# Gate and up products of two feed-forward halves by seven block products instead of eight, with blocks of 256 tokens

## The chip, the cores and the metric

The kernel runs on one core of a Trainium2 chip. The metric is the device time of one execution in microseconds (us), the median over several runs. TensorE (PE) does the matrix products into PSUM; VectorE (DVE), ScalarE (ACT) and GpSimd (POOL) do the element-wise work; SyncE (SP) issues the transfers.

## The reference

Two layers over 1024 tokens with 1024 features: a recurrent block (Hawk) in layer 0, an RWKV-7 time mixing in layer 1, and after each a dense feed-forward and a gated per-layer embedding ("ple"). The change touches the feed-forward:

```python
def swiglu(x, w_in, w_out):
    gu = x @ w_in
    gate, up = jnp.split(gu, 2, axis=-1)
    return (jax.nn.silu(gate) * up) @ w_out
...
    h = h + swiglu(rms_norm(h, norm_ffn[i]), ffn_w_in[i], ffn_w_out[i])
    ple = (p[i] @ ple_w_proj[i]) * jax.nn.sigmoid(rms_norm(h, norm_ple[i]) @ ple_w_gate[i])
    h = h + ple
```

The inner width of the feed-forward is 2816, which is 22 tiles of 128.

## The kernel before

Features lie on the 128 partitions and tokens along the free dimension. The 1024 tokens are two halves of 512 (index t), so each layer has two feed-forward halves, four in all. The features of one half are eight tiles (index k).

Every product is made exact enough by splitting both operands into a high part (rounded to the matmul's type) and a low part (the remainder): `mm3` issues three matmuls for each k, high by high, high by low and low by high, each with a 128x128 weight and 512 columns. A weight tile arrives in `raw` (SP's queue), ScalarE casts its high part into `whl` and GpSimd subtracts to get the low part (`load_w`, L238 and L239). In the two regions where a second half of the hidden state fits beside the first (`extra`), `raw` has 2+2 buffers and `whl` 4+4.

A feed-forward half (`ffn`) goes over the 22 tiles f in groups of 2, 4, 4, 4, 4, 4. For each f it makes the gate product `pg` and the up product `pu` (24 matmuls each), then `silu(pg) * pu`, split into the tile `hid`. After each group the output products `ops` (`out_proj`, eight columns n, three matmuls for each f of the group) are added into the hidden state h (L390). In the last group the squares of h are summed as well (L301), and the norm for the next stage starts (`nxt`).

A norm for the whole half (`norm_xn`) needs one matmul `nps` that sums over the partitions, two activations that give `rstd`, and then for each k one multiply on VectorE (L317) and one split (cast on ScalarE, subtraction on VectorE, L290). Where `raw` is given (`raw_x`), the unnormed h is split instead, and `rstd` is applied behind the product.

The scheduler of the framework fixes each engine's order when the program is built, by priorities in program order and by its own idea of what is ready; on the chip each engine takes its instructions strictly in that order. Two of the four feed-forward halves concern us: the first half of layer 0, behind Hawk, and the second half of layer 1, near the end.

## Time and profile before

| | |
|---|---|
| median of 3 runs | 3099.32 us |
| lowest and highest | 3097.59 and 3109.37 us |
| the profiled execution, its own time | 3106.82 us |
| its span | 3105.0 us |
| matmuls in it | 16904 |
| PE busy in the span | 2958.3 us |

The span runs from the first to the last instruction; the profiled execution's own time is 1.8 us above it. A matmul's busy time is modelled, since matmuls overlap; what one costs in a row of them is read from the distance of starts.

### The profile page before, as it was taken

Reading aid. Unit: us, or ns where it says so; the run is one execution under the profiler, and the core shown is the slowest. Engines: PE = TensorE matmul, PEld = TensorE weight load, DVE = VectorE, ACT = ScalarE, POOL = GpSimd, SP = SyncE. Lnnn points to the kernel's source line nnn. Section 1 sums busy time; section 2 is a strip of 40 time slices with the busy share of each in tenths; the row PEclk is TensorE's granted clock in tenths of the full one; section 3 lists DMA queues with packets and bytes.
Section 4 is the critical chain, followed back from the end, with each engine's and each line's share of the span. In section 5 each row is a group of like instructions: output and inputs, shape, how many; then the busy total and the mean of one; then the engine's idle time right before and its main releaser. Section 6 shows DMA issues by size and latency. Waiting matters only on the chain. (4 is left out here: it accounts for less than half of the span.)

```text
span 3105.0 us, 45886 instructions
## 1 busy us (share of the span) xinstructions
PE 2958.3 (95%) x16904; PEld 2292.7 (74%) x16904; DVE 1677.9 (54%) x2950; ACT 1438.3 (46%) x2565; POOL 1282.7 (41%) x1080
## 2 busy tenths in 40 slices
PE   5999999999999999999998999999999999999998
PEld 3777778888776777777776667776767777888886
DVE  8756771111563266576678565777866456222145
ACT  5564752222555443444465774454344445322244
POOL 5111134444445444343434344434333355544445
PEclk9999999999998999999999999999999999999999
DMA  3211123333335464333323366423323252333323
GB/s 126 60 36 53 50 79 105 94 94 95 98 126 179 158 190 128 89 111 98 114 91 98 119 204 198 125 85 111 100 88 100 70 185 91 103 95 95 95 81 109
DMA packets 223968, 336.04 MB, mean 108 GB/s; under 512 B 56960, under 2 KB 75136, under 8 KB 223744
## 3 DMA queue, kind: packets, MB, share of 16 engines
q1 hardware_dynamic: 223456, 332.75, 34.9%
q8 instruction: 133, 2.18, 0.3%
q14 instruction: 91, 0.75, 0.1%
q10 hardware_dynamic: 288, 0.37, 0.0%
HBM read 278.24 MB, written 54.79 MB: 107 GB/s over the span
## 5 line engine op out<-in xcount | busy, mean ns | idle before, releaser
L239 POOL TENSOR_TENSOR whl<-raw,whl 128x512 fp32r<-128x512 f32 (+2 forms) x818 | 1061.8, 1303 | 1410.4 <-ACT whl L238 1319.8
L238 ACT CAST whl<-raw 128x512 fp32r<-128x512 f32 (+2 forms) x818 | 482.2, 593 | 851.5 <-PE ops L115 226.2
L115 PE MATMUL ops<-hid,whl 128*128 128x512 f32 x2112 | 523.8, 401 | 13.8 <-DVE hid L290 6.4
L115 PE MATMUL pg<-xn,whl 128*128 128x512 f32 (+1 forms) x2184 | 522.9, 392 | 4.4 <-ACT whl L238 1.9
L115 PEld LDWEIGHTS pg<-xn,whl 128*128 128x128 f32 x2184 | 405.2, 188 | 98.9 <-issue 4.3
L115 PEld LDWEIGHTS ops<-hid,whl 128*128 128x128 f32 x2112 | 392.6, 189 | 113.8 <-DVE hid L290 12.5
L115 PE MATMUL pu<-xn,whl 128*128 128x512 f32 x1584 | 385.9, 396 | 3.1 <-ACT xn L289 1.4
L115 PEld LDWEIGHTS pu<-xn,whl 128*128 128x128 f32 x1584 | 296.0, 189 | 72.0 <-DVE xn L290 2.1
L115 PE MATMUL pps<-mix,whl 128*128 128x512 f32 x1152 | 301.3, 412 | 11.9 <-ACT mix L289 5.1
L390 DVE TENSOR_TENSOR h<-h,ops 128x512 f32<-128x512 f32 x256 | 173.9, 685 | 210.6 <-PE ops L115 208.7
L555 DVE TENSOR_TENSOR sg<-sg,pu 128x512 f32<-128x512 f32 x88 | 60.4, 686 | 396.0 <-PE pu L115 395.4
L115 PEld LDWEIGHTS pps<-mix,whl 128*128 128x128 f32 x1152 | 217.7, 193 | 75.1 <-issue 7.7
L115 PE MATMUL pg<-raw,whl 128*128 128x512 f32 x720 | 198.0, 415 | 0.0
L115 PEld LDWEIGHTS pg<-raw,whl 128*128 128x128 f32 x720 | 134.4, 193 | 34.4 <-issue 3.8
L241 POOL TENSOR_SCALAR whl<-raw 128x512 fp32r<-128x512 f32 (+2 forms) x84 | 58.7, 704 | 217.6 <-PE rps L115 69.7
L115 PE MATMUL pu<-raw,whl 128*128 128x512 f32 x528 | 141.4, 406 | 0.0
L115 PE MATMUL rps<-xn,whl 128*128 128x512 f32 x480 | 123.4, 405 | 16.3 <-ACT xn L289 10.5
L115 PEld LDWEIGHTS rps<-xn,whl 128*128 128x128 f32 x480 | 91.9, 193 | 42.8 <-issue 12.0
L115 PE MATMUL gps<-xn,whl 128*128 128x512 f32 x480 | 117.9, 400 | 0.0
L115 PE MATMUL ops<-m,whl 128*128 128x512 f32 x480 | 114.4, 396 | 0.8 <-ACT m L289 0.8
L115 PEld LDWEIGHTS pu<-raw,whl 128*128 128x128 f32 x528 | 96.1, 188 | 23.8 <-issue 2.6
L115 PEld LDWEIGHTS gps<-xn,whl 128*128 128x128 f32 x480 | 92.3, 192 | 21.4 <-issue 0.5
(277 smaller groups left out, 4027.2 us busy)
## 6 DMA issues: line engine op xcount, KB each, us to landing
raw<-in_ffn_in SPq DMA_DIRECT2D x352, 256.0 KB, 2.6
raw<-in_ffn_out SPq DMA_DIRECT2D x152, 256.0 KB, 2.6
raw<-in_rkv SPq DMA_DIRECT2D x96, 256.0 KB, 3.0
raw<-in_ple_gate SPq DMA_DIRECT2D x64, 256.0 KB, 2.6
raw<-in_w_in SPq DMA_DIRECT2D x48, 256.0 KB, 2.8
h<-h SPq DMA_DIRECT2D x32, 256.0 KB, 3.5
raw<-in_ffn_out SPq DMA_DIRECT2D x48, 128.0 KB, 2.1
raw<-in_w_o SPq DMA_DIRECT2D x24, 256.0 KB, 2.7
```

The lines of the kernel that those rows point to most:

```text
L115: self.nc.tensor.matmul(out, lhsT=lhsT, rhs=rhs, start=start, stop=stop)
L238: nc.scalar.copy(hl[:rows, 0, :w], raw[:rows, :w])
L239: nc.gpsimd.tensor_sub(hl[:rows, 1, :w], raw[:rows, :w], hl[:rows, 0, :w].bitcast(F32))
L241: nc.gpsimd.tensor_scalar(hl[:rows, 0, :w], raw[:rows, :w], 1.0, 0.0, ALU.mult, ALU.add)
L390: nc.vector.tensor_add(hs, hs, ps)
L555: nc.vector.tensor_mul(sg, sg, pu)
```

## The change

The gate and up products of one f are seen as a 2x2 block product: rows gate and up, inner blocks k = 0..3 and k = 4..7, columns the first and the last 256 tokens. `ffn_s` makes it with seven block products (`prod`, each 4 k x 3 matmuls of 256 columns), with Winograd's order of sums. The sums of weight blocks (S1 to S4) are made by VectorE for every f in `strassen_w`, and seven weight blocks are split instead of four tiles. The sums of activation blocks (T1 to T4) are made once for each half in `norm_s`. The products share three PSUM tiles `sA`, `sB` and `sC`, whose intermediate values are copied or added out in 256-column pieces; the last two products of an f are done between those of the next f. The output products of a group are issued behind the first f of the next group.

Around it: Hawk's end no longer norms the second half, which `norm_later` does during the last output products of the first half. In layer 1 the ple columns of half 0 are no longer split around the feed-forward of half 1, and the norm ahead of the last ple is applied behind the product (`raw`), for which `ple_last` multiplies by `rn`. `raw` and `whl` get 2+4 and 4+7 buffers, and one more activation tile is there in the second region. 

```diff
-            raw = self.ring("raw", [128, 512], F32, 2, 2)
+            raw = self.ring("raw", [128, 512], F32, 2, 4)
...
-            hl = self.ring("whl", [128, 2, 512], F32R, 4, 4)
+            hl = self.ring("whl", [128, 2, 512], F32R, 4, 7)
...
+    def norm_later(self, t, gname, gi, keep=False):
+        r = self.rstd(t)
+        self.rn[t] = None
+        xn = [self.xq("xn", "xb") for _ in range(4)]
+        self.xn[t] = xn
+        def some(k0):
+            for k in (k0, k0 + 1):
...
+    def norm_s(self, t, gname, gi):
+        nc = self.nc
+        r = self.rstd(t)
+        self.rn[t] = None
+        b11 = self.xq("xs", "xb")
+        t12 = [self.xq("xs", "xb") for _ in range(2)]
+        b2 = [self.xq("xs", "xb"), self.xq("xs")]
+        t34 = [self.xq("xs", "xb"), self.xq("xs", "hid")] if self.nxb > 4 else [self.xq("xs") for _ in range(2)]
+        def two(x):
+            return x.rearrange("p (b s) -> p b s", s=TH // 2)
+        def put(dst, src, lo):
+            nc.scalar.copy(dst[0], src)
+            lo.tensor_sub(dst[1], src, dst[0].bitcast(F32))
+        a, b = slice(0, TH // 2), slice(TH // 2, TH)
+        for k in range(4):
+            x, y, u, v = (self.t2("xn") for _ in range(4))
+            self.scaled(x, k, t, gname, gi, r)
+            self.scaled(y, k + 4, t, gname, gi, r)
+            q = b11.rearrange("p i a (b s) -> p i (a b) s", s=TH // 2)
+            put([q[:, i, k, :] for i in range(2)], x[:, a], nc.vector)
+            nc.vector.tensor_sub(u[:, a], x[:, b], x[:, a])
+            nc.vector.tensor_sub(u[:, b], y[:, b], u[:, a])
+            nc.gpsimd.tensor_sub(v[:, a], y[:, b], x[:, b])
+            nc.vector.tensor_sub(v[:, b], y[:, a], u[:, b])
+            for q, src, lo in ((t12, u, nc.vector), (b2, y, nc.vector), (t34, v, nc.gpsimd)):
+                q = q[k // 2].rearrange("p i a (b s) -> p i a b s", s=TH // 2)
+                put([q[:, i, :, k % 2, :] for i in range(2)], two(src), lo)
...
+    def strassen_w(self, g, u):
+        nc = self.nc
+        g0, u0, u1, g1 = raw = [self.ring("raw", [128, 512], F32, 2, 4) for _ in range(4)]
+        for x, src in zip(raw, (g[:, 0:512], u[:, 0:512], u[:, 512:1024], g[:, 512:1024])):
+            nc.sync.dma_start(x, src)
+        s1, s2, s3, s4 = (self.te("ws") for _ in range(4))
+        def split(x, lo):
+            hl = self.ring("whl", [128, 2, 512], F32R, 4, 7)
+            nc.scalar.copy(hl[:, 0, :], x)
+            lo.tensor_sub(hl[:, 1, :], x, hl[:, 0, :].bitcast(F32))
+            return lambda k, i: hl[:, i, k * 128 : k * 128 + 128]
+        w = {"A11": split(g0, nc.gpsimd)}
+        nc.vector.tensor_add(s1, u0, u1)
+        w["S1"] = split(s1, nc.gpsimd)
+        nc.vector.tensor_sub(s2, s1, g0)
+        w["S2"] = split(s2, nc.vector)
+        nc.vector.tensor_sub(s4, g1, s2)
+        w["A12"] = split(g1, nc.gpsimd)
+        w["S4"] = split(s4, nc.vector)
+        nc.vector.tensor_sub(s3, g0, u0)
+        w["S3"] = split(s3, nc.gpsimd)
+        w["A22"] = split(u1, nc.gpsimd)
+        return w
+    def ffn_s(self, l, t, nxt, groups, mid=None, raw=None):
+        nc, A = self.nc, self.A
+        a, b = slice(0, TH // 2), slice(TH // 2, TH)
+        def prod(ps, w, x, start, stop):
+            for k in range(4):
+                wh, wl, xh, xl = w(k, 0), w(k, 1), x(k, 0), x(k, 1)
+                for i, (p, q) in enumerate(((wh, xh), (wh, xl), (wl, xh))):
+                    nc.tensor.matmul(ps[:, a], lhsT=p, rhs=q, start=start and k + i == 0, stop=stop and k == 3 and i == 2,
+                                     skip_group_check=True)
...
+        def finish(last):
+            w, pa, s4, sg, fq, fj = last
+            def seven():
+                prod(pa, w["S3"], X["T3"], False, False)
+                nc.vector.tensor_add(s4[:, a], pa[:, a], s4[:, a])
+            def four():
+                prod(pa, w["A22"], X["T4"], False, True)
+                nc.vector.tensor_mul(sg[:, b], sg[:, b], s4[:, a])
+                nc.vector.tensor_mul(sg[:, a], sg[:, a], pa[:, a])
+                self.split(fq[:, 0, fj, :], fq[:, 1, fj, :], sg)
+            return seven, four
...
+        for g in groups:
+            for i in range(g):
+                if i % 2 == 0:
+                    q = self.xq("hid", "hid" if nq % 2 and self.nxb == 4 else None)
+                    nq += 1
+                hd[f + i] = q, i % 2
+                w = self.strassen_w(A["ffn_in"][l, f + i], A["ffn_in"][l, NF + f + i])
+                pa, pb, pc = self.ps("sA"), self.ps("sB"), self.ps("sC")
+                st, s4, sg = (self.t2(x) for x in ("st", "s4", "sg"))
+                seven, four = finish(hold) if hold else (lambda: None,) * 2
+                prod(pa, w["A11"], X["B11"], True, False)
+                nc.scalar.copy(st[:, a], pa[:, a])
+                seven()
+                prod(pb, w["S1"], X["T1"], True, False)
+                nc.scalar.copy(s4[:, a], pb[:, a])
+                prod(pa, w["S2"], X["T2"], False, False)
+                nc.scalar.copy(st[:, b], pa[:, a])
+                four()
+                prod(pc, w["A12"], X["B21"], True, True)
+                nc.vector.tensor_add(sg[:, a], pc[:, a], st[:, a])
+                prod(pb, w["S4"], X["B22"], False, True)
+                nc.vector.tensor_add(sg[:, b], pb[:, a], st[:, b])
+                nc.scalar.activation(sg, sg, AF.Silu)
+                hold = w, pa, s4, sg, q, i % 2
+                if todo is not None:
+                    out(*todo)
+                    todo = None
+            todo = f, g, f + g == NF
+            f += g
+        seven, four = finish(hold)
+        seven()
+        four()
+        if mid is not None:
+            mid()
+        out(*todo)
...
-            nc.scalar.activation(sg, pg, AF.Exp, scale=-1.0)
+            nc.vector.tensor_mul(sg, pg, self.rn[t][:, s])
+            nc.scalar.activation(sg, sg, AF.Exp, scale=-1.0)
...
-        K.hawk(lambda t: K.norm_xn(t, "norm_ffn", 0, t == 1))
+        K.hawk(lambda t: K.norm_s(t, "norm_ffn", 0) if t == 0 else None)
...
-        K.ffn(0, (0,), norm_ple)
+        K.ffn_s(0, 0, norm_ple, (2, 4, 4, 4, 4, 4), lambda: K.norm_later(1, "norm_ffn", 0, True))
...
-    extra(ctx)
+    extra(ctx, 5)
...
-    K.rwkv_out(1, 0, KD, True, lambda t: K.norm_xn(t, "norm_ffn", 8))
-    K.ple(1, (0,), K.final, ph, 0, 4)
-    K.ffn(1, (1,), lambda t: K.norm_xn(t, "norm_ple", 8))
-    K.ple(1, (0,), K.final, ph, 4, KD)
+    K.rwkv_out(1, 0, KD, True, lambda t: K.norm_s(t, "norm_ffn", 8))
+    K.ple(1, (0,), K.final, ph)
+    K.ffn_s(1, 1, lambda t: K.raw_norm(t, False), (2, 4, 4, 4, 4, 4), raw=("norm_ple", 8))
```

The order shows what moves on PE. In the middle of a feed-forward half of before, PE has two products of 24 matmuls for each f, and `ops` behind four f:

```order
L115 MATMUL pg<-xn,whl 128x512 x24
L115 MATMUL pu<-xn,whl 128x512 x24
L115 MATMUL pg<-xn,whl 128x512 x24
L115 MATMUL pu<-xn,whl 128x512 x24
L115 MATMUL ops<-hid,whl 128x512 x96
```

In the change the output products of a group stand behind the first f of the next; then comes one f: 24 matmuls into `sA` (the first product of this f and the sixth of the one before), 12 into `sB`, 24 into `sA` (the third of this, the last of the one before), and 12 each into `sC` and `sB`:

```order
L115 MATMUL ops<-hid,whl 128x512 x96
L660 MATMUL sA<-xs,whl 128x256 x24
L660 MATMUL sB<-xs,whl 128x256 x12
L660 MATMUL sA<-xs,whl 128x256 x24
L660 MATMUL sC<-xs,whl 128x256 x12
L660 MATMUL sB<-xs,whl 128x256 x12
```

So an f has 84 matmuls of 256 columns where it had 48 of 512.

At the end of Hawk's output products (`ops<-m`, the last four columns of the second half), where the first feed-forward half begins, PE has before:

```order
L115 MATMUL ops<-m,whl 128x512 x38
L115 MATMUL pu<-xn,whl 128x512 x36
L115 MATMUL nps<-acc,ones 128x512
L115 MATMUL pg<-xn,whl 128x512 x48
L115 MATMUL pu<-xn,whl 128x512 x12
L115 MATMUL ops<-hid,whl 128x512 x48
```

and in the change, where `xs` are the activation blocks from `norm_s`:

```order
L115 MATMUL ops<-m,whl 128x512 x38
L660 MATMUL sA<-xs,whl 128x256 x6
L660 MATMUL sB<-xs,whl 128x256 x3
L660 MATMUL sC<-xs,whl 128x256 x3
L660 MATMUL sB<-xs,whl 128x256
L660 MATMUL sC<-xs,whl 128x256 x3
L660 MATMUL sA<-xs,whl 128x256 x4
L660 MATMUL sB<-xs,whl 128x256 x2
L660 MATMUL sA<-xs,whl 128x256 x2
L660 MATMUL sB<-xs,whl 128x256 x5
L660 MATMUL sA<-xs,whl 128x256 x2
L660 MATMUL sB<-xs,whl 128x256
```

The products of the first two f are interleaved there, and the `nps` of the second half has gone from this place; it stands behind the last f of the half.

On VectorE the same place (h_93 is the second half's hidden state, h_86 the first's) reads before:

```order
L390 TENSOR_TENSOR h_93<-h_93,ops 128x512
L317 SCALAR_TENSOR_TENSOR xn<-h_86,vec,rstd 128x512 x3
L290 TENSOR_TENSOR xn<-xn 128x512 x3
L317 SCALAR_TENSOR_TENSOR xn<-h_86,vec,rstd 128x512 x3
L290 TENSOR_TENSOR xn<-xn 128x512 x3
L317 SCALAR_TENSOR_TENSOR xn<-h_86,vec,rstd 128x512 x2
L301 TENSOR_TENSOR acc<-acc,sq 128x512
L290 TENSOR_TENSOR xn<-xn 128x512 x2
```

and in the change the same norm is mixed with the block sums (L608 to L611) and the low parts of seven blocks (L599); of its four rounds this is the first and the start of the second:

```order
L407 TENSOR_TENSOR h_93<-h_93,ops 128x512
L317 SCALAR_TENSOR_TENSOR xn<-h_86,vec,rstd 128x512 x2
L599 TENSOR_TENSOR xs<-xn,xs 128x256
L608 TENSOR_TENSOR xn<-xn 128x256
L407 TENSOR_TENSOR h_93<-h_93,ops 128x512
L609 TENSOR_TENSOR xn<-xn 128x256
L317 SCALAR_TENSOR_TENSOR xn<-h_86,vec,rstd 128x512
L611 TENSOR_TENSOR xn<-xn 128x256
L599 TENSOR_TENSOR xs<-xn,xs 128x2x256 x2
L317 SCALAR_TENSOR_TENSOR xn<-h_86,vec,rstd 128x512
L599 TENSOR_TENSOR xs<-xn,xs 128x256
L608 TENSOR_TENSOR xn<-xn 128x256
```

What was 16 instructions of 512 columns for the eight k is now 16 of 512 and 16 of 256 columns, with three of the four `h_93` additions between them.

## Rows read from the trace of the kernel before

**Rows 1.** The page: busy us (share of the span) and instructions of each engine.

```profile
PE 2958.3 (95%) x16904; PEld 2292.7 (74%) x16904; DVE 1677.9 (54%) x2950; ACT 1438.3 (46%) x2565; POOL 1282.7 (41%) x1080
```

**Rows 2.** Windows: busy us (instructions) in two stretches, granted clock, DMA share, GB/s.

```profile
400.00:500.00 100.00, 97.66 (x408) 77.12 (x407) 54.27 (x72) 44.77 (x76) 42.21 (x33) 0.98 0.32 100
...
2700.00:2800.00 100.00, 99.21 (x435) 81.16 (x434) 19.96 (x25) 29.02 (x48) 47.05 (x37) 1.00 0.31 95
```

**Rows 3.** Timeline of PE, one group of four f: start, us, xcount [idle before].

```profile
2739.97 5.66 PE L115 MATMUL pg<-xn,whl 128*128 128x512 f32 x24
2745.46 5.60 PE L115 MATMUL pu<-xn,whl 128*128 128x512 f32 x24
...
2783.70 2.46 PE L115 MATMUL ops<-hid,whl 128*128 128x512 f32 x10
2786.55 19.88 PE L115 MATMUL ops<-hid,whl 128*128 128x512 f32 x86 [0.39 <-DVE hid L290]
2806.27 5.66 PE L115 MATMUL pg<-xn,whl 128*128 128x512 f32 x24
```

**Rows 4.** Timeline of the last us, where matmuls have 256 columns.

```profile
3084.25 3.01 PE L115 MATMUL pg<-xn,whl 128*128 128x256 f32 x24
...
3087.09 0.86 PE L115 MATMUL pq<-ph,whl 128*128 128x256 f32 x6
3087.79 0.59 PE L115 MATMUL nps<-acc,ones 128*128 128x256 f32 x2
...
3089.32 0.42 DVE L635 TENSOR_TENSOR sg<-sg,pq 128x256 f32<-128x256 f32 x1 [2.00 <-ACT sg L634]
```

**Rows 5.** Groups by line and shape, PE: busy us, mean ns.

```profile
L115 PE MATMUL pg<-xn,whl 128*128 128x256 f32 x48 | 6.5, 288 | 0.0
```

**Rows 6.** The same view of POOL, ACT and DVE: busy us, mean ns | idle before.

```profile
L239 POOL TENSOR_TENSOR whl<-raw,whl 128x512 fp32r<-128x512 f32 x718 | 976.2, 1364 | 1257.0 <-ACT whl L238 1183.2 <-issue 28.8 <-DVE h L390 13.8
```
```profile
L238 ACT CAST whl<-raw 128x512 fp32r<-128x512 f32 x718 | 442.0, 618 | 777.4 <-PE ops L115 208.9 <-PE pu L115 123.1 <-PE pg L115 108.7
...
L238 ACT CAST whl<-raw 128x256 fp32r<-128x256 f32 x96 | 38.1, 402 | 73.1 <-PE ops L115 17.3 <-PE pg L115 16.8 <-DMA raw<-in_w_o 14.7
```
```profile
L390 DVE TENSOR_TENSOR h<-h,ops 128x512 f32<-128x512 f32 x256 | 173.9, 685 | 210.6 <-PE ops L115 208.7
```

**Rows 7.** Timeline of POOL and DVE inside a feed-forward half, layer 0.

```profile
745.87 1.30 POOL L239 TENSOR_TENSOR whl<-raw,whl 128x512 fp32r<-128x512 f32 x1 [1.46 <-ACT whl L238]
...
746.57 1.14 DVE L290 TENSOR_TENSOR hid<-sg,hid 128x512 fp32r<-128x512 f32 x1 [0.69 <-ACT hid L289]
```

**Rows 8.** Timeline of PE, then DVE, then POOL: Hawk's end, first feed-forward half.

```profile
417.68 9.38 PE L115 MATMUL ops<-m,whl 128*128 128x512 f32 x38
426.89 4.56 PE L115 MATMUL pu<-xn,whl 128*128 128x512 f32 x18
432.90 0.50 PE L115 MATMUL pu<-xn,whl 128*128 128x512 f32 x1 [1.44 <-ACT xn L289]
434.12 0.96 PE L115 MATMUL pu<-xn,whl 128*128 128x512 f32 x3 [0.71 <-DVE xn L290]
```
```profile
404.71 0.68 DVE L390 TENSOR_TENSOR h<-h,ops 128x512 f32<-128x512 f32 x1
...
420.10 2.68 DVE L317 SCALAR_TENSOR_TENSOR xn<-h,vec,rstd 128x512 f32<-128x512 f32 x3 [0.66 <-ACT rstd L313]
422.70 1.89 DVE L290 TENSOR_TENSOR xn<-xn 128x512 fp32r<-128x512 f32 x3
424.50 4.19 DVE L317 SCALAR_TENSOR_TENSOR xn<-h,vec,rstd 128x512 f32<-128x512 f32 x3
...
433.38 1.82 DVE L290 TENSOR_TENSOR xn<-xn 128x512 fp32r<-128x512 f32 x2
```
```profile
404.65 1.30 POOL L239 TENSOR_TENSOR whl<-raw,whl 128x512 fp32r<-128x512 f32 x1 [2.46 <-ACT whl L238]
...
423.36 4.11 POOL L239 TENSOR_TENSOR whl<-raw,whl 128x512 fp32r<-128x512 f32 x2 [2.46 <-ACT whl L238]
```

More of the change, by code (lines that the diff above doesn't have):

```diff
@@ L204, in xq @@
             return self.xp.tile([128, 2, 2, TH], F32R, tag="xq", name=nm, bufs=6)
-        return self.ep.tile([128, 2, 2, TH], F32R, tag=ext, name=nm, bufs={"xb": 4, "hid": 2}[ext])
+        return self.ep.tile([128, 2, 2, TH], F32R, tag=ext, name=nm, bufs={"xb": self.nxb, "hid": 2}[ext])
     def ring(self, tag, shape, dt, bufs, more):
@@ L330, in norm_xn @@
         self.pause(4500)
+    def norm_later(self, t, gname, gi, keep=False):
[5 more added lines that the diff above has]
+            for k in (k0, k0 + 1):
+                x = self.t2("xn")
+                self.scaled(x, k, t, gname, gi, r)
+                if keep:
+                    self.nc.sync.dma_start(self.xn_d[k], x)
+                self.split(*self.xs(k, t), x)
+        self.items = [lambda k0=k0: some(k0) for k0 in range(0, KD, 2)]
     def raw_x(self, k, t, gname, gi):
@@ L562, in ffn, with pair @@
             f0 += g
+    def norm_s(self, t, gname, gi):
[14 more added lines that the diff above has]
+            x, y, u, v = (self.t2("xn") for _ in range(4))
+            self.scaled(x, k, t, gname, gi, r)
+            self.scaled(y, k + 4, t, gname, gi, r)
[8 more added lines that the diff above has]
+                put([q[:, i, :, k % 2, :] for i in range(2)], two(src), lo)
+        def pair(q, j):
+            return lambda k, i: q[k // 2].rearrange("p i a (b s) -> p i a b s", s=TH // 2)[:, i, j, k % 2, :]
+        self.xsb = {
+            "B11": lambda k, i: b11.rearrange("p i a (b s) -> p i (a b) s", s=TH // 2)[:, i, k, :],
+            "T1": pair(t12, 0), "T2": pair(t12, 1), "B21": pair(b2, 0), "B22": pair(b2, 1),
+            "T3": pair(t34, 0), "T4": pair(t34, 1),
+        }
@@ new lines, in ffn_s, with out @@
+    def ffn_s(self, l, t, nxt, groups, mid=None, raw=None):
[7 more added lines that the diff above has]
+                                     skip_group_check=True)
+        X = self.xsb
+        f, hd, hold, todo = 0, {}, None, None
+        def finish(last):
[9 more added lines that the diff above has]
+            return seven, four
+        def out(f0, g, last):
+            self.out_proj(
+                lambda n: self.load_w(A["ffn_out"][l, n, :, f0 * 128 : (f0 + g) * 128], g * 128),
+                g, lambda k, t: (hd[f0 + k][0][:, 0, hd[f0 + k][1], :], hd[f0 + k][0][:, 1, hd[f0 + k][1], :]),
+                (t,), last=last, nxt=nxt, raw=raw if last else None)
+        nq = 0
+        for g in groups:
[33 more added lines that the diff above has]
+        out(*todo)
@@ L569, in ple_in @@
             s = slice(t * TH, (t + 1) * TH)
-            q = self.xq("ph", "hid" if len(ts) == 2 and t == 1 else None)
+            q = self.xq("ph", "hid" if self.ep is not None and t == 1 else None)
             for k in range(2):
@@ L1298, in tile_trunk, with extra @@
     nc = tc.nc
-    def extra(c):
+    def extra(c, nxb=4):
+        K.nxb = nxb
         K.ep = c.enter_context(tc.tile_pool(name="ep", bufs=1))
@@ L1442 @@
     arrays = layout({k: np.asarray(v) for k, v in inputs.items()})
-    nc = bacc.Bacc("TRN2", target_bir_lowering=False, num_devices=1)
+    nc = bacc.Bacc("TRN2", target_bir_lowering=False, num_devices=1, dynamic_dma_scratch_size=1024)
     A = {n: nc.dram_tensor("in_" + n, a.shape, mybir.dt.from_np(a.dtype), kind="ExternalInput").ap()
```

## The prediction

> **What bounds the kernel now.** I read the page's busy shares first: PE is busy for 95% of the span, every other engine for 54% or less [rows 1]. Then the windows: in the middle of a feed-forward half PE is at 99% and at the full clock, while DVE has 20%, ACT 29%, POOL 47% and the transfers 31% of their time [rows 2]. So in the two halves that change PE alone sets the pace, and what a matmul costs there is read from the distance of starts, since busy times overlap. Two products of 24 matmuls start 5.49 us apart; four f take 2783.70 - 2739.97 = 43.73 us, so one f 10.93 us; the group with its 96 output matmuls takes 66.30 us [rows 3]. That is 228 ns for 512 columns. PE waits only 0.39 us in the group, for the low part of the last `hid`.
>
> **The gain on PE.** The order shows 84 matmuls of 256 columns for each f in place of 48 of 512, and 22 f in each of two halves, 44 in all. Half as many columns pay only if such a matmul costs about half. The trace has some at its very end: 24 take 3087.09 - 3084.25 = 2.84 us, 118.3 ns each, and the next six 0.70 us, 117 ns each [rows 4]. With 118.3 ns an f costs 9.94 us, 0.99 less, and 44 of them give **-43.7 us**. The bounds: exactly half of the 512-column distance, 113.9 ns, gives 9.57 us and -60 us. The busy time of the group of 48 divided by its count, 135 ns [rows 5], which counts edges and gaps twice, gives 11.34 us and +18 us. I take the distance of starts of the 24, because they are the same kind of stream and long enough. A rule of the Trainium skill speaks against the change: the page TensorE: Matmul & The Clock Gate, section "Why this matters for your kernels", wants all dimensions at 512 or more for a good share of the peak. The rows disagree so far: the short matmuls lose about 4% against half a long one, not more. The same page, "Back-to-back issue gap", has columns over 2.4 GHz plus 2.5 ns for a lone gap; as an estimate that is 109 and 216 ns, and the gain would be 52 us; both measured distances are longer.
>
> **What the other engines get.** Durations: a GpSimd subtraction of 512 columns 1.30 us [rows 7] (1.36 in the mean), an ACT cast 0.62 and one of 256 columns 0.40, a DVE operation on 512 columns 0.69 [rows 6], on 256 columns 0.42 [rows 4]. For each f, POOL has five subtractions where it had four, 6.5 us; ACT seven casts, three 256-column copies, silu and the cast of `hid` (0.6 us each), 6.8 us; DVE four sums of weight blocks, two low parts, the low part of `hid` (seven of 0.69) and five operations on 256 columns, 6.9 us where it had two of 0.69. All are below the 9.94 us of PE. Over a group (4 x 9.94 plus the unchanged 22.57 us of output products, 62.3 us) POOL has 36.4, DVE 33.2 and ACT 32.0 us with the output weights. Transfers move the same bytes in 6% less time, 31% of the engines. So on their sums none becomes the bound; this is the cover under which all of it costs nothing.
>
> But DVE and POOL hold each other up. A DVE subtraction with both inputs in SBUF starts at 746.57, while a POOL one runs until 747.17, and takes 1.14 us in place of 0.69 [rows 7]; three DVE multiplies took 4.19 us beside two POOL subtractions that took 4.11 in place of 2.6. An addition that reads PSUM kept its 0.68 us beside a POOL one [rows 8]. If POOL is active 65% of the time, a DVE operation of the first kind costs 0.69 + 0.65 x 0.45 = 0.98 us, and DVE has 7 x 0.98 + 2.1 = 9.0 us for an f: 90% full while no output products run. PE leaves some room: after S3 (24 matmuls of other products, 2.84 us) DVE must have added the result before the last product may go on in `sA`; the copies of the first and second results have 24 matmuls too, or more. Behind two held-up operations (2 x 1.14 + 0.42 = 2.7 us) it just fits. I take 0.15 us for each f, **+6.6 us**; the bounds are 0 and the rivals below.
>
> **The start of the first half.** This is the one place where work is moved onto PE's path. Before, the norm of eight k took DVE from 420.10 to 435.2, 15.1 us for 17 operations of some 0.66 us, 11.2 us undisturbed, so 1.35 times as long, and PE, which had finished Hawk's output products at 426.89, waited 1.44 + 0.71 = 2.1 us for it [rows 8]. Now DVE has, up to the last block part, 16 operations of 512 and 16 of 256 columns, three additions, one low part and one sum: 8 x 0.69 + 8 x 0.63 + 16 x 0.42 + 5 x 0.69 = 20.7 us, or with the same factor 28 us, so it ends between 440.8 and 448. Every product needs all four k. By the order, PE can do 66 matmuls of the first two f without the last part, 7.8 us. So it waits 6.1 to 13.4 us, 4 to 11.3 more than before. A stretch of such waits has lowered the granted clock here already (0.98 in the mean of the 100 us around it [rows 2]); I add 2 us for a deeper drop. I take **+10 us**, near the long end since POOL has some ten subtractions in that time. The second changed half starts behind eight ple columns of 30 matmuls (6.8 us each), which hide its norm: nothing; without that cover it would cost the same again.
>
> **Smaller terms.** The output products now stand behind another f, so the wait for `hid` at the end of a group goes: five in each half, 0.39 us each, **-3.9 us**. What is late next there is the addition of the previous f, counted above. At the end of each half the last two products have nothing between them: a matmul's end, an addition of 0.42 us and two handovers, about 1 us, **+2 us**. `ple_last` multiplies once more in each 256-column piece, 0.42 us with its handover, on the last chain: **+1 us**. The norm of the second half moves under the last output products of the first (22.6 us): DVE has 8 x (0.69 + 0.63) for it plus 16 x 0.69 that were there, 21.6 us; nothing, up to +5 if it is late, when the first `pg` of the next half waits. The last ple's norm becomes a factor behind the product, 8 multiplies under 6.8 us columns: nothing. More `raw` and `whl` buffers: nothing, since PE hardly waits for weights.
>
> **Sum.** -43.7 + 10 + 6.6 - 3.9 + 3 = -28.0 us. The profiled execution took 3106.8 us, the median of the runs shown is 3099.3, 7.5 less. From 3106.8 that gives 3078.8; on the scale of the median **3071 us**.
>
> **The rivals.**
> (a) The matmuls go as half of the long ones and nothing waits inside an f: -60 + 4 - 3.9 + 3 = -57, 3042 to 3058 us. For it: the unused shares. Against it: the measured 118 ns.
> (b) Late evictions: where DVE's queue holds an S3 addition behind three held-up operations (3.4 us and its own 0.42 against 2.84), PE waits about 1 us; on half of the 44 f this is 22 us in place of 6.6: 3087, with the drop at Hawk's end at its worst 3095. Nearly no change. For it: DVE 90% full between output products. Against it: the weight work is about one f ahead, so DVE may also sit idle and take additions at once.
> (c) The other side: DVE and POOL take turns on everything. An f then needs 7 x 0.69 + 6.5 = 11.3 us of turns. Over a group this is 4 x 11.3 + 8 x 1.3 = 55.7 us of 62.3, so it fits if the weights run ahead during the output products; eleven `whl` buffers hold one and a half f. If they do not, each f costs 11.3 in place of 9.94, +61 us: 3071 - 7 + 61 = 3125 us, slower. It decides from the point where an f costs 9.94 + (43.7 - 9) / 44 = 10.73 us: above it the change loses. The Trainium skill has a rule for this: SBUF — State Buffer, "Who interferes with whom", says that a DVE instruction with two SBUF inputs and a GpSimd one that reads SBUF exclude each other for a whole instruction. By that rule nothing of the turns overlaps and this rival is the one to fear; the 1.14 us agrees with it.
> That the products are still eight is excluded by the order.
>
> **How the numbers follow.** Forecast (3058 to 3083): 0.59. (a): 0.14. (b): 0.14. (c): 0.13. About 0.5%, 15.5 us, can be told from no change by this measurement. Faster by more than that, below 3083.8: the forecast and (a), 0.73. Same: (b), nearly all, 0.14. Slower: (c), 0.13. The range leaves out the far end of (a) below 3044 and (c) but for its mild cases above 3100.
>
> **What would show it.** Right: 24 matmuls of `sA` and the next product 2.8 us apart, an f in 9.9 to 10.2 us, groups in 62 to 63.5 us; at Hawk's end PE waits for `xs` of 6 to 13 us; no waits for `hid` in a group. Wrong: PE waiting for `s4` or `st` in every f (b); PE waiting for `whl` from POOL with POOL and DVE busy together (c); a distance above 125 ns without waits, which would mean that the short matmuls are bound by something that 24 in a row at the end did not show.

## The result, and the profile after

The changed kernel takes 3134.72 us (median of 4 runs, 3129.06 to 3137.27) against 3100.57 us before (four runs, the three shown above and one more), a ratio of 1.0103 with a 95% interval of [1.0078, 1.0128]: 1% slower, where 3071 us was forecast. The profiled execution took 3137.27 us, its span 3135.5 us at a granted clock of 0.971 in the mean.

The page's busy shares, to be read beside [rows 1], and the windows of [rows 2] again:

```profile
PE 2938.4 (94%) x18488; PEld 2346.3 (75%) x18488; DVE 1988.6 (63%) x3423; ACT 1556.2 (50%) x2844; POOL 1380.9 (44%) x1140
```
```profile
400.00:500.00 100.00, 88.22 (x514) 78.05 (x513) 82.25 (x111) 48.35 (x92) 49.79 (x40) 0.93 0.19 59
2700.00:2800.00 100.00, 87.31 (x616) 81.08 (x616) 69.81 (x94) 48.75 (x94) 59.89 (x46) 0.93 0.35 112
```

Each window line gives the busy us (and instructions) of PE, PEld, DVE, ACT and POOL, then the granted clock, the share of the transfers and GB/s. PE was at 99% in the second window and is at 87%, at a granted clock of 0.93. DVE has gone from 20 to 70%, POOL from 47 to 60%.

The timeline of PE in the first half, three f in a row, answers to [rows 3] (last bracket: idle before, and what ended it):

```profile
561.80 3.01 PE L660 MATMUL sA<-xs,whl 128*128 128x256 f32 x24
...
566.07 1.57 PE L660 MATMUL sA<-xs,whl 128*128 128x256 f32 x12
571.17 2.93 PE L660 MATMUL sA<-xs,whl 128*128 128x256 f32 x12 [3.53 <-DVE s L672]
573.89 2.76 PE L660 MATMUL sC<-xs,whl 128*128 128x256 f32 x12
...
586.72 1.58 PE L660 MATMUL sB<-xs,whl 128*128 128x256 f32 x12
588.14 2.99 PE L660 MATMUL sA<-xs,whl 128*128 128x256 f32 x24
590.97 1.58 PE L660 MATMUL sB<-xs,whl 128*128 128x256 f32 x12
...
596.62 1.58 PE L660 MATMUL sB<-xs,whl 128*128 128x256 f32 x12
...
601.16 1.21 PE L115 MATMUL ops<-hid,whl 128*128 128x512 f32 x4 [0.65 <-DVE hid L290]
```

Undisturbed, an f takes 596.62 - 586.72 = 9.90 us, and 24 matmuls 590.97 - 588.14 = 2.83 us: what was forecast. But in the f ahead of it PE waits 3.53 us, and the 12 matmuls behind that wait need 573.89 - 571.17 = 2.72 us, where 12 took 1.42 in the undisturbed f (588.14 - 586.72): half speed. The wait for `hid` at the group's end is not gone either, it is 0.65 us.

DVE and POOL at that wait, from a timeline of all engines:

```profile
567.76 1.35 DVE L640 TENSOR_TENSOR ws<-raw 128x512 f32<-128x512 f32 x1 [5.33 <-DMA raw<-in_ffn_in]
...
568.65 1.58 POOL L636 TENSOR_TENSOR whl<-raw,whl 128x512 fp32r<-128x512 f32 x1
569.03 1.74 DVE L636 TENSOR_TENSOR whl<-ws,whl 128x512 fp32r<-128x512 f32 x1
570.70 0.41 DVE L672 TENSOR_TENSOR s<-sA,s 128x256 f32<-128x256 f32 x1
```

The eviction L672, for which PE stands (`s` is the tile `s4`, printed without its number), adds the product of S3, whose matmuls are the second half of the 24 at 561.80. They end 2.83 us later, at 564.6, if they take as long as the 24 of the undisturbed f, and from then on it could start. But in DVE's queue it is behind a weight sum that waits for its load until 567.76, 5.33 us after DVE's last operation. Then this sum takes 1.35 and a low part 1.74 us; either would be 0.69 without the POOL operation beside it. PE has finished its other 24 matmuls at 567.64. So some 3 us of the eviction's delay are the load, 2.9 us the two held-up operations; with these at 0.69 PE would, as an estimate from these rows, still have waited some 2 us.

Where the time went, from the timelines of PE: the start of Hawk's last output matmul; from there to the last output matmul of the first half; from there to the end of layer 1's `rwkv_out`; from there to the last matmul (the last half with its ple columns).

```
us            to Hawk's end   first half   middle   last part     sum
before              426.7        373.8     1810.7      486.1     3097.3
after               429.3        377.1     1827.4      493.6     3127.5
forecast change         0         -9.5          0      -18.5      -28
change               +2.7         +3.3      +16.7       +7.5      +30.2
```

PE's waits say where the halves lose (us in total, times, longest). The first half before, then after:

```profile
PE ops L115 <- DVE hid L290: 1.7, 5, 0.3
PE pu L115 <- ACT xn L289: 1.4, 1, 1.4
PE pu L115 <- DVE xn L290: 0.9, 2, 0.7
```
```profile
PE sA L660 <- DVE s L672: 7.6, 4, 3.5
PE sA L660 <- ACT st L700: 6.2, 5, 1.9
PE sA L660 <- DVE xs L599: 2.6, 2, 1.5
PE ops L115 <- DVE hid L290: 2.2, 3, 0.9
PE sB L660 <- ACT xs L598: 1.9, 1, 1.9
...
```

The last part before, then after:

```profile
PE nps L115 <- ACT sq L637: 4.0, 2, 3.6
PE ops L115 <- DVE hid L290: 2.0, 5, 0.4
PE nps L115 <- DVE acc L301: 1.3, 3, 0.6
```
```profile
PE sA L660 <- DVE s L672: 6.0, 5, 2.0
PE nps L115 <- DVE acc L301: 5.9, 2, 5.6
...
PE sA L660 <- ACT st L700: 3.2, 3, 2.6
PE sA L660 <- POOL whl L636: 2.7, 1, 2.7
...
```

The waits for `st` belong to the same queue: its copies stand in ACT's queue behind casts and a silu for which ACT itself waits for DVE (the longest, 1.91 us, ends with a copy at 513.39, behind a silu that had waited for DVE's L710).

In the first half all waits add up to 4.0 us before and 22.4 after, 18.4 more. Matmuls at half speed cost the rest: 99 of them some 95 ns more each, 9.4 us, against 2.3 us before. 18.4 + 7.1 - 21.9 (22 f, 0.99 us each) = +3.6, for a measured +3.3. Of the 99, 57 lie in the first 25 us, where PE waits for the input's blocks, and 27 behind the 3.53 us wait; behind each of the other waits inside the half at most three matmuls were slow. In the last part the waits go from 7.3 to 27.5 us, and some 50 matmuls at half speed cost 5 us: +3.3 of the measured +7.5; for the other 4 us, which lie in matmuls that start late without a wait on record, I have no cause.

### The profile page after: what moved, and what is told of

Its sections match the earlier page's. It is cut to its first block, busy times and chain, and to the rows that moved or that the text cites. A ratio compares the mean times of both kernels' runs of the same rounds, so it can differ in the third digit from the quotient of the medians.

```text
span 3135.5 us, 50071 instructions
## 1 busy us (share of the span) xinstructions
PE 2938.4 (94%) x18488; PEld 2346.3 (75%) x18488; DVE 1988.6 (63%) x3423; ACT 1556.2 (50%) x2844; POOL 1380.9 (44%) x1140
## 5 line engine op out<-in xcount | busy, mean ns | idle before, releaser
L239 POOL TENSOR_TENSOR whl<-raw,whl 128x512 fp32r<-128x512 f32 (+1 forms) x642 | 827.6, 1297 | 1022.8 <-ACT whl L238 944.3
L238 ACT CAST whl<-raw 128x512 fp32r<-128x512 f32 (+1 forms) x642 | 373.9, 586 | 487.5 <-PE ops L115 74.2
L660 PE MATMUL sA<-xs,whl 128*128 128x256 f32 x2112 | 277.7, 286 | 29.8 <-DVE s L672 13.6
L660 PEld LDWEIGHTS sA<-xs,whl 128*128 128x128 f32 x2112 | 264.0, 193 | 38.1 <-DVE s L672 16.9
L636 POOL TENSOR_TENSOR whl<-raw,whl 128x512 fp32r<-128x512 f32 x132 | 192.5, 1460 | 169.3 <-ACT whl L635 152.1
L115 PE MATMUL pg<-raw,whl 128*128 128x512 f32 (+1 forms) x936 | 241.4, 401 | 0.0
L115 PE MATMUL pg<-xn,whl 128*128 128x512 f32 x912 | 228.4, 400 | 4.1 <-ACT whl L238 1.9
L115 PEld LDWEIGHTS pg<-xn,whl 128*128 128x128 f32 x912 | 170.3, 189 | 47.9 <-issue 3.4
L660 PE MATMUL sB<-xs,whl 128*128 128x256 f32 x1056 | 144.1, 285 | 3.2 <-ACT xs L598 1.9
L115 PE MATMUL pu<-xn,whl 128*128 128x512 f32 x528 | 134.3, 400 | 0.9 <-POOL whl L239 0.7
```

Of the source, the lines that this page charges most:

```text
L115: self.nc.tensor.matmul(out, lhsT=lhsT, rhs=rhs, start=start, stop=stop)
L238: nc.scalar.copy(hl[:rows, 0, :w], raw[:rows, :w])
L239: nc.gpsimd.tensor_sub(hl[:rows, 1, :w], raw[:rows, :w], hl[:rows, 0, :w].bitcast(F32))
L636: lo.tensor_sub(hl[:, 1, :], x, hl[:, 0, :].bitcast(F32))
L660: nc.tensor.matmul(ps[:, a], lhsT=p, rhs=q, start=start and k + i == 0, stop=stop and k == 3 and i == 2, skip_group_check=True)
```

## The experiments

All times are medians, ratios are to the kernel before, run on the same chip, with their 95% interval. Its median lay between 3103.1 and 3104.7 us in them, 2.5 to 4 us above that of the result, so a difference between medians of two runs is uncertain by some us. Stretches inside a kernel ("the first half takes") are read from its one profiled execution. "A" and "B" are the theories of the text put down before each run.

**One half, or the buffers alone.** First the side change by itself, on the kernel before:

```diff
-            raw = self.ring("raw", [128, 512], F32, 2, 2)
+            raw = self.ring("raw", [128, 512], F32, 2, 4)
...
-            hl = self.ring("whl", [128, 2, 512], F32R, 4, 4)
+            hl = self.ring("whl", [128, 2, 512], F32R, 4, 7)
...
-    nc = bacc.Bacc("TRN2", target_bir_lowering=False, num_devices=1)
+    nc = bacc.Bacc("TRN2", target_bir_lowering=False, num_devices=1, dynamic_dma_scratch_size=1024)
```

> The kernel before with only the side changes of buffers: six buffers for the raw weights instead of four, eleven for their split parts instead of eight, and the smaller scratch for DMA descriptors. Theory A (the loss comes from the product scheme itself, its queues and its starts): within 10 us of before, 3090 to 3110. Rival B (the side changes shift the loads and cost by themselves, which would explain the 14 us lost outside the two halves): 3112 or more.

3113.27 us, 1.0027 [1.0012, 1.0042]: some 8 us slower. By the time alone that is B; by the ratio, which would put it at 3109 where the result was taken, it is still in A's range. So the buffers cost something clear of noise, but not surely what B said. Its timeline shows the place of most of it, the last feed-forward of layer 1's first tokens: 5.5 us are lost in this one group of output products. Before, in it, and in the changed kernel:

```profile
2551.43 10.61 PE L115 MATMUL ops<-hid,whl 128*128 128x512 f32 x38 [2.52 <-ACT hid L289]
```
```profile
2558.82 11.87 PE L115 MATMUL ops<-hid,whl 128*128 128x512 f32 x38 [5.68 <-ACT hid L289]
```
```profile
2574.09 10.68 PE L115 MATMUL ops<-hid,whl 128*128 128x512 f32 x38 [5.40 <-ACT hid L289]
```

Then one half at a time, the other as before (the edit of the first half, against the kernel before):

```diff
-    K.hawk(lambda t: K.norm_xn(t, "norm_ffn", 0, t == 1))
+    K.hawk(lambda t: K.norm_s(t, "norm_ffn", 0) if t == 0 else None)
...
-    K.ffn(0, (0,), norm_ple)
+    K.ffn_s(0, 0, norm_ple, (2, 4, 4, 4, 4, 4), lambda: K.norm_later(1, "norm_ffn", 0, True))
```

> Seven products only in the first half (layer 0); the second half, its start and the last columns as before. Theory A (each half loses by its own waits; the first had lost some 9 us by its end and about 14 more are lost by later waits that the shifted loads cause): 3107 to 3125. Rival B (what is lost outside belongs to the second half's larger pool of buffers): 3100 to 3109, with the programs in step from 900 us on.

3128.17 us, 1.0082 [1.0067, 1.0097], above both; its first half takes 377.1 us, as in the changed kernel. A holds in kind; it loses more than A said.

> Seven products only in the second half (layer 1); the first as before. Theory A: the second half lost some 7 us from its start to the end of the program, so 3104 to 3112, with the wait for the final norm's sum (5 to 6 us) and the half-speed stretches in its first 30 us as in the changed kernel. Rival B (its start is only late because the loads come late after the first half's shift): at or under 3085, as the predicted gain of some 20 us comes out.

3121.78 us, 1.0059 [1.0044, 1.0074], above both. B falls: with the program nearly in step ahead of it (2.3 us late at Hawk's end, 4.5 at 2616), the last part takes 494.9 us, 8.8 more than before. So buffers, first half and second half each lose by themselves: 8 us, and beyond that, by the ratios, some 17 and 10; the changed kernel's own ratio gives 32. Place by place it doesn't add up as well: the middle lost 8.6 us with the buffers alone and 2.5 with the buffers and the second half.

**What is late inside the halves.** The changed kernel without its weight sums:

```diff
-        s1, s2, s3, s4 = (self.te("ws") for _ in range(4))
+        s1, s2, s3, s4 = u0, g0, u0, g1
...
-        nc.vector.tensor_add(s1, u0, u1)
...
-        nc.vector.tensor_sub(s2, s1, g0)
...
-        nc.vector.tensor_sub(s4, g1, s2)
...
-        nc.vector.tensor_sub(s3, g0, u0)
```

> The changed kernel with the four weight sums S1 to S4 left out: the raw blocks are split and multiplied in their place, so the output isn't the reference's, and the matmuls are as many as before. Theory A (evictions stand behind the weight sums in VectorE's queue, and the sums wait for loads and collide with GpSimd): most of the 30 us of waits inside the two halves goes, groups of four f come down to 62 to 64 us throughout, and the time falls by 20 to 35 us, to 3100 to 3115. Rival B (the waits come from the starts, the clock and the splits on GpSimd): it falls by less than 10 us, 3125 or more.

3083.87 us, 0.9935 [0.991, 0.996]: 51 us less, more than A said. The halves take 353.3 and 470.7 us, 20.5 and 15.4 less than before; the forecast had 9.5 and 18.5. So the products do pay where the sums don't stand in the way. What it is about the sums was asked in three ways. Their loads:

```diff
-        nc.vector.tensor_add(s1, u0, u1)
+        nc.vector.tensor_add(s1, c, c)      (c: a block of B11 in SBUF; s2, s3, s4 likewise)
```

> The changed kernel with its four weight sums kept at full size on VectorE, but reading a block of the normed input that stays in SBUF in place of the loaded gate and up blocks, so the output isn't the reference's. Queue and work on VectorE stay, only the wait for the loads goes. Theory A1 (evictions wait behind sums that wait for a load): most of the 51 us between the changed kernel and the one without sums comes back, 3085 to 3100. Rival A2 (the sums' own time on VectorE, with what GpSimd does to it, makes the evictions late): 3115 to 3135.

3141.71 us, 1.0124 [1.0103, 1.0146], above both: the wait for loads is gone and nothing is gained. But DVE now waits 37.3 us from 460 to 812 us for POOL, which still reads the buffers of sums, where it waited 33.5 for loads: one stall has come in place of another. And a sum of the first f must now wait for the normed input, so that the first output products stand 55.1 us behind Hawk's end in place of 42.5. So the run shows that the loads aren't the only stall that makes evictions late; it does not show that a stall costs nothing. Their time:

```diff
-        nc.vector.tensor_add(s1, u0, u1)
-        w["S1"] = split(s1, nc.gpsimd)
+        nc.vector.tensor_add(s1[:, o], u0[:, o], u1[:, o])      (o: one column)
+        w["S1"] = split(u0, nc.gpsimd, s1)      (the ACT copy adds that column; S2, S4, S3 likewise)
...
```

> The changed kernel with each of the four weight sums cut to one column of 512: the order in VectorE's queue stays, each sum still waits for its loads, and ScalarE's copy of the raw block still waits for the sum (it adds that column), so the output isn't the reference's. Only the sums' time on VectorE goes, some 4 us per f. Theory A1 (the wait for the loads in the queue): 3115 to 3135, little changed. Rival A2 (the sums' time and their collisions): 3085 to 3100.

3098.89 us, 0.9983 [0.9968, 0.9999], 36 us less with the order in DVE's queue kept: A2. From 460 us to the half's end DVE still waits 36.4 us for loads, the longest time 4.1, and PE waits for `st` twice, 1.5 us in all. And what makes their time long:

```diff
+            if lo is nc.gpsimd:
+                return lambda k, i: hl[:, 0, k * 128 : k * 128 + 128]
             lo.tensor_sub(hl[:, 1, :], x, hl[:, 0, :].bitcast(F32))
```

> The changed kernel without the five low parts per f that GpSimd makes of the weights (the high part is multiplied in their place, so the output isn't the reference's); VectorE's queue and the loads as they are. If the collisions of GpSimd with VectorE's operations (0.69 us alone, up to 1.8 beside it) carry the loss: 3085 to 3105. If it is the loads or the bare length of VectorE's queue: 3115 or more.

3085.53 us, 0.9947 [0.9929, 0.9965], 49 us less, with every DVE operation still there. The waits of DVE (us, times, longest) and its groups by line, from 460 to 800 us, in the changed kernel, and then in this one:

```profile
DVE ws L640 <- DMA raw<-in_ffn_in: 33.5, 15, 5.3
```
```profile
L636 DVE TENSOR_TENSOR whl<-ws,whl 128x512 fp32r<-128x512 f32 x40 | 36.9, 926 | 11.9 <-ACT whl L635 11.7
L640 DVE TENSOR_TENSOR ws<-raw 128x512 f32<-128x512 f32 x19 | 19.5, 1028 | 37.2 <-DMA raw<-in_ffn_in 33.5 <-issue 2.3 <-POOL whl L636 1.4
L676 DVE TENSOR_TENSOR sg<-sg,s 128x256 f32<-128x256 f32 x21 | 18.2, 865 | 1.3 <-ACT sg L711 0.2
```
```profile
DVE ws L642 <- DMA raw<-in_ffn_in: 28.9, 17, 2.4
```
```profile
L638 DVE TENSOR_TENSOR whl<-ws,whl 128x512 fp32r<-128x512 f32 x38 | 26.2, 688 | 15.4 <-ACT whl L635 15.3
```

DVE still waits 28.9 us for loads here, though at most 2.4 at a time, and from 460 us to the half's end at 777 PE has no wait on record (one of 5.8 us for `acc` comes behind it). The low part of the sums fell from 926 to 688 ns. So in these two runs a stall in DVE's queue costs PE little or nothing, as the operations behind it are short enough to catch up; stall and held-up operations together make the evictions late. POOL's low parts also keep the raw buffers in use, which this run can't tell from the collision.

**Buffers.** Ten buffers for raw weights, paid with two of those for split parts:

```diff
-            raw = self.ring("raw", [128, 512], F32, 2, 4)
+            raw = self.ring("raw", [128, 512], F32, 2, 8)
...
-            hl = self.ring("whl", [128, 2, 512], F32R, 4, 7)
+            hl = self.ring("whl", [128, 2, 512], F32R, 4, 5)
```

> The changed kernel with ten buffers for raw weights instead of six, paid with nine buffers for split parts instead of eleven; the result is the reference's. Theory A1: a sum finds its loads there, 10 to 30 us less, 3105 to 3125. Rival A2: the loads were not what is waited for in the end, or the fewer split parts cost as much: within 8 us of the changed kernel or slower, 3127 to 3150.

3093.35 us, 0.9969 [0.9953, 0.9984]: 41 us less than the changed kernel, more than A1 said, and faster than before, by buffers alone. The first half and the last part become 15.7 and 12.8 us shorter. DVE's waits for loads go from 33.5 to 17.2 us, but those for POOL from 2.7 to 17.0, and its operations stay as long. From 460 to 800 us PE waits for DVE's evictions only once:

```profile
PE nps L115 <- DVE acc L301: 6.5, 1, 6.5
...
PE sA L660 <- DVE s L672: 0.6, 1, 0.6
```

The second half of that edit without the first (six raw buffers, nine split ones):

> The changed kernel with its six raw buffers and only nine buffers for split parts instead of eleven: the other half of the edit of the kernel with ten raw buffers. Theory A (the loads' buffers carry that gain): no better than the changed kernel, 3128 to 3145. Rival B (fewer split parts keep the preparation of weights from running ahead into VectorE's queue, and that is the gain): 3095 to 3115.

3109.53 us, 1.0022 [1.0011, 1.0033]: B: 25 of the 41 us come from having *fewer* split buffers; A falls. Of the 30 us between the two profiled executions 12 lie in the middle, 7.6 and 6.2 in the first half and the last part, 4 ahead of them. The raw buffers, on top of that, give the other 16. And ten raw and nine split buffers in the kernel before:

> The kernel before with the same buffers as the faster version: ten for raw weights, nine for split parts, and the smaller scratch for descriptors. Theory A (before had its loads in time; the buffers matter only where sums stand between load and split): within 6 us of before, 3097 to 3109. Rival B (they help or hurt any product): more than 8 us either way, and the comparison of the seven products has to be made against this kernel.

3099.85 us, 0.9984 [0.9973, 0.9995], within what A said. So of the 0.3% by which the kernel with ten raw buffers is faster, half would be there without the seven products.

**The starts and the ends.** The final norm of the first 512 tokens behind the second half, on the version with ten raw buffers:

```diff
-    K.ple(1, (0,), K.final, ph)
-    K.ffn_s(1, 1, lambda t: K.raw_norm(t, False), (2, 4, 4, 4, 4, 4), raw=("norm_ple", 8))
+    K.ple(1, (0,), lambda t: None, ph)
+    K.ffn_s(1, 1, lambda t: K.raw_norm(t, False), (2, 4, 4, 4, 4, 4), raw=("norm_ple", 8))
+    K.final(0)
```

> The kernel with ten raw buffers, and the final norm of the first 512 tokens (its sum on TensorE, the table switch on ScalarE, its eight multiplications on VectorE) moved from the start of the second half to behind it. The half's first 30 us had 12 us of waits and 13.7 us at half clock. Theory A (the final norm holds the evictions and the splits back there): 8 to 16 us under the kernel with ten raw buffers, 3077 to 3086. Rival B (the first weight sums are late there anyway, behind the last columns' own work): 0 to 5 us, 3088 to 3094.

3085.91 us, 0.9941 [0.9923, 0.9958], 7.4 us less. The time is just inside A, the difference falls between A and B. It is the fastest kernel of those that give the whole result. The half's start in the changed kernel (PE, then DVE), and in this one (PE):

```profile
2695.09 0.50 PE L660 MATMUL sA<-xs,whl 128*128 128x256 f32 x2 [1.39 <-ACT whl L635]
2698.32 2.50 PE L660 MATMUL sA<-xs,whl 128*128 128x256 f32 x10 [2.72 <-POOL whl L636]
2706.37 2.08 PE L115 MATMUL nps<-acc,ones 128*128 128x512 f32 x2 [5.55 <-DVE acc L301]
...
```
```profile
2709.87 5.49 DVE L317 SCALAR_TENSOR_TENSOR fin<-h,vec,rstd 128x512 f32<-128x512 f32 x5 [3.55 <-ACT rstd L313]
...
2715.88 4.08 DVE L317 SCALAR_TENSOR_TENSOR fin<-h,vec,rstd 128x512 f32<-128x512 f32 x3
```
```profile
2668.37 2.93 PE L660 MATMUL sA<-xs,whl 128*128 128x256 f32 x12 [5.92 <-ACT st L700]
```

The wait for the norm's sum and its multiplications are gone; one wait of 5.92 us stays, for a copy that stands in ACT's queue behind squares and sigmoids of the last ple columns, for which ACT itself waits for DVE. B holds for that part.

At the start, two ways to make the blocks of the input sooner, and at the end of the first half one for the norm of the other tokens:

```diff
-            for q, src, lo in ((t12, u, nc.vector), (b2, y, nc.vector), (t34, v, nc.gpsimd)):
+            for q, src, lo in ((t12, u, nc.vector), (b2, y, nc.gpsimd), (t34, v, nc.gpsimd)):
```

> The kernel with ten raw buffers and the final norm behind the half, and of the seven blocks of the input the low parts of two (B21 and B22, eight instructions at the start of each half) on GpSimd in place of VectorE. Theory A (VectorE's own work, some 22 us, sets the start of the first half): 2 to 4 us less than without this move. Rival B (GpSimd, which makes three of the blocks and the weights' low parts there, and stops VectorE while it works, becomes the later one): the same or up to 5 us more.

3091.47 us, 0.9962 [0.9948, 0.9976], 5.6 us more than without it, a little over B's range; A falls. The first half takes 363.8 us in place of 361.6; most of the rest lies in the middle, where nothing was changed.

```diff
-                self.split(*self.xs(k, t), x)
+            self.split(*self.xs(k, t), x, True)      (low part on GpSimd)
...
-        self.items = [lambda k0=k0: some(k0) for k0 in range(0, KD, 2)]
+        self.items = [lambda k=k: some(k) for k in range(KD)]
```

> On the kernel with ten raw buffers and the final norm behind the half: the norm of the second 512 tokens at the end of the first half is made one block per output column instead of two in each of the first four, with its low parts on GpSimd. In every version with the new first half, TensorE waits 5.7 to 6.5 us behind that half for the sum of squares, with 6.8 us at half clock behind it; before it waited 0.39. Theory A (the norm's multiplications, new at this place, stand ahead of the residual's sums in VectorE's queue): the wait falls to 1 to 3 us and the time by 3 to 9 us, to 3077 to 3083. Rival B (VectorE has more to do there than eight columns give time for, wherever it is done, and GpSimd stops it): the wait stays over 4 us, the time within 3 us of 3086 or above.

3087.73 us, 0.9947 [0.9932, 0.9963]: no change, and the wait is 6.57 us. B. One column of this stretch:

```profile
786.25 1.74 POOL L290 TENSOR_TENSOR xn<-xn 128x512 fp32r<-128x512 f32 x1
...
786.76 0.67 DVE L406 TENSOR_TENSOR h<-h,ops 128x512 f32<-128x512 f32 x1
...
787.36 1.19 DVE L317 SCALAR_TENSOR_TENSOR xn<-h,vec,rstd 128x512 f32<-128x512 f32 x1
...
787.95 1.74 POOL L239 TENSOR_TENSOR whl<-raw,whl 128x512 fp32r<-128x512 f32 x1
788.47 1.77 DVE L301 TENSOR_TENSOR acc<-acc,sq 128x512 f32<-128x512 f32 x1
...
795.99 1.22 PE L115 MATMUL nps<-acc,ones 128*128 128x512 f32 x1 [6.57 <-DVE acc L301]
```

DVE needs 0.67 + 1.19 + 1.77 = 3.6 us for a column that PE does in 2.8. With the norm's low part added to its weights' low parts POOL is busy through the whole column, and DVE pays for it: its sum takes 1.77 us in place of 0.69.

```diff
...
+        for k in range(4):
+            self.scaled(xk[k], k, t, gname, gi, r)
+            put([q[:, i, k, :] for i in range(2)], xk[k][:, a], nc.vector)
         for k in range(4):
-            x, y, u, v = (self.t2("xn") for _ in range(4))
-            self.scaled(x, k, t, gname, gi, r)
+            x, (y, u, v) = xk[k], (self.t2("xn") for _ in range(3))
             self.scaled(y, k + 4, t, gname, gi, r)
...
```

> As the run before it, and at the start of each half the block B11, which the first product needs, is made for all four groups of rows ahead of the other six blocks. Theory A (the order within the start's work costs TensorE part of its 10 us of waits there): 3 to 6 us less than without it. Rival B (the start is bound by the sum of VectorE's work, some 22 us): within 3 us.

3095.85 us, 0.9968 [0.9952, 0.9984], 8 us more than the run before it. The first product runs at once, and then PE waits 16.53 us for weights, whose sums stand behind the whole of the input's work on DVE:

```profile
425.76 1.45 PE L661 MATMUL sA<-xs,whl 128*128 128x256 f32 x11
443.75 0.79 PE L661 MATMUL sB<-xs,whl 128*128 128x256 f32 x2 [16.53 <-ACT whl L636]
```

Both theories fall. Neither order nor a second engine shortened this start; its work on DVE would have to be less, which wasn't tried.

## Why the prediction was wrong

Between the forecast change and the measured one lie 58 us on the table of stretches: 12.8 in the first half, 26.0 in the last part, 16.7 in the middle, 2.7 ahead of them. For the two changed stretches it is DVE's queue beside POOL that the prediction had wrong: without POOL's low parts they come to 36.4 us below before, where 28 were forecast. The middle stays 14.9 us above before in that run too; there it is terms that were put at nothing, some 7 us for the norm made later and some 8 for the buffers.

**The gain on PE** (-43.7): right. 24 matmuls take 2.83 us and an f 9.90 where nothing waits, and without POOL's low parts the first half is 23.3 us shorter than before, start included. The rule of the Trainium skill that wants all dimensions at 512 or more (TensorE: Matmul & The Clock Gate, "Why this matters for your kernels") did not decide this case: 256 columns cost 118 ns, 4% above half of the 228 ns of 512.

**What the other engines get** (+6.6): the step that failed. The durations were right: the seven DVE operations of 512 columns came to 0.92 us in the mean of their groups, against 0.98 worked out. A multiplication of `sg` by `s`, put at 0.42, took 0.87; the sum for an f is 9.0 us, as forecast. But the step weighed a 90% full DVE against two operations ahead of an eviction, and no stall. In the queue there was a sum that waited for its load, with one or two held-up operations behind it, and 2.84 us of margin were not enough. PE's waits for `s` and `st` are 13.8 us in the first half and 9.2 in the last part, 23.0 in place of 6.6, in 17 waits. Behind two of them, of 3.53 and 2.60 us, a stretch of matmuls runs at half speed, which the step left out. That is rival (b), in its place and with its 22 us; (b)'s time of 3087 failed by the terms below. Rival (c), turns of DVE and POOL, came nearest to the time (3125) and its mechanism lengthens the queue, as the run without POOL's low parts shows, but it is not what PE waits for: only one wait for POOL, of 2.7 us. The Trainium skill's rule on the shared port (SBUF — State Buffer, "Who interferes with whom") agrees with the 1.77 and 0.67 us of the column above: the sum with two SBUF inputs is held while POOL's subtraction runs, the addition that reads PSUM is not.

**The start of the first half** (+10): about right. Waits for `xs` are 6.4 us, the short end of the 6.1 to 13.4 worked out, against 2.3 before, and half speed there costs some 5 us against 2.

**The start of the second half** (nothing): wrong, and for another reason than its cover. The ple columns do hide `norm_s`. Not counted was that the final norm, which before stood at another place, now falls among the first products: 5.55 us of wait, 9.6 us of DVE for `fin` and a stretch at half speed. Waits for split weights there (`whl`) are 4.9 us. Moving the norm gave 7.4 us.

**The norm made later** (nothing, up to +5): wrong. DVE's sum of 21.6 us was made with 0.69 us for each sum of squares. With POOL beside it DVE falls behind, and PE waits for `acc` 5.72 us where it waited 0.39, and the granted clock is at half from 812.9 to 819.7, so that the first matmuls behind the wait are slow too. Before, then after:

```profile
803.53 1.13 PE L115 MATMUL nps<-acc,ones 128*128 128x512 f32 x2 [0.39 <-DVE acc L301]
```
```profile
814.90 2.07 PE L115 MATMUL nps<-acc,ones 128*128 128x512 f32 x2 [5.72 <-DVE acc L301]
```

From the half's end to the output products that end at 945 us 11 us are lost. Some 7 of them lie ahead of these products and are this norm's. The other 4 lie in the products themselves, for a wait of 2.6 us for `hid` that the kernel before has too with the new buffers alone (2.68, against 0.19): most of that is the buffers'. The middle's other 6 us are gains and losses at many places, of which I can name only the wait at 2574, again with the buffers alone.

**The buffers** (nothing): wrong; +8.5 us in the kernel before, and 41 us hang on their numbers in the changed one. "PE hardly waits for weights" was true and beside the point, since buffers also change what DVE's queue waits for (with ten raw ones 17.2 us for loads in place of 33.5, and 17.0 for POOL); why PE then waits less for DVE is not shown.

**Waits for `hid`** (-3.9): wrong. They are 2.2 and 2.6 us against 1.7 and 2.0.

What stays open: why eleven split buffers are worse than nine. The order of DVE's instructions differs between the two, but no run took order and buffers apart.

## What to carry to other kernels

When a change moves work to an engine that was 20% busy, the sum of its time says little; look at what will stand in its queue ahead of the operations that the busy engine waits for, and how long these become beside the other engine on the same memory. Look for that margin in buffers first, and measure their number, since more was not always better here: the same seven products go from 1.0% slower to 0.6% faster with ten and nine buffers and one norm moved, 0.4% against the kernel before with the same buffers. Where a stage's end or start is filled with new work, count each instruction that was there already at its disturbed price.

## What was not expected of the hardware

A wait can cost PE more than its length: behind the 3.53 us of waiting above, 12 matmuls took 2.72 us in place of 1.42. A window of the 6.8 us there (busy us of each engine, then the granted clock) has it at half, 1.2 GHz; in the 5 us ahead it was full:

```profile
565.00:570.00 5.00, 2.64 (x23) 2.43 (x21) 2.24 (x2) 2.25 (x5) 3.94 (x3) 1.00 0.35 102
570.50:577.30 6.80, 6.13 (x28) 6.14 (x29) 4.89 (x10) 1.71 (x3) 0.00 (x0) 0.50 0.25 77
```

In the changed kernel's first half matmuls at half speed cost 9.4 us on top of 22.4 us of waits, some 5 of them at its start.

Fewer buffers made a kernel faster: nine in place of eleven for the split weights, 25 us. The cause is open.
